# One decoder step on one core: the S5 direct term moved into the Toeplitz matrix, and an S5 plan with other prices

## The chip, the cores and the metric

The kernel runs as one launch on one core of a Trainium2 chip. The metric is device time in microseconds (us), the median of several executions. TensorE (PE, with its weight loads as PEld), VectorE (DVE), ScalarE (ACT), GpSimd (POOL) and SyncE (SP) each work through a queue of their own, in order. All DMAs of this kernel are issued from SP's queue.

## What is computed

One layer of a hybrid decoder, for 512 prompt tokens and 8 sample tokens, which the kernel holds side by side as 520 columns. The input projection feeds two branches: an S5 state space model (64 groups of 16 channels with 64 complex states) and a Mamba-2 SSD. The change touches the S5 branch alone:

```python
h_re, h_im = associative_scan(...)                  # h_t = abar h_(t-1) + bbar u_t
y = einsum("ghn,blgn->blgh", c_re, h_re) - einsum("ghn,blgn->blgh", c_im, h_im)
y = y + d_skip * u32                                # the direct term
ya = gelu(y)
out = ya * sigmoid(ya @ w_glu + b_glu)
```

Behind it come the SSD branch, gates on both, an output projection, and a SwiGLU feed-forward part.

## The kernel before, in words

**Big products.** Every projection is cut into tiles of 128 output channels by 520 columns. A weight tile of 128x1024 is loaded, split by ACT into a rounded high part (`whi`, line 755 `acp`) and by DVE into the rest (`wlo`, line 699 `vtt`), and PE multiplies it with the high and low parts of the activations (`hi`, `lo`): six matmuls of 260 columns for each of 8 slices of the contraction, 48 for a tile, all recorded at line 782 (`mm`). The results go to one of two PSUM tiles, `pm`, and are read out by ACT or DVE. These products run in a fixed list of tiles: 8 tiles `u` (the S5 input), a small `dt` tile, then sixteen gate tiles and four SSD groups of ten tiles (`B`, `C`, four `xs`, four `z`). `CUT` (line 513) says how many gate tiles stand ahead of the first group and behind each group: with `[12, 14, 16, 16, 16]` it is 12 ahead, 2 behind the first group and 2 behind the second. Then come `glu`, `bs5`, `bssd`, `wo`, the feed-forward tiles `fg`/`fu` and `fo`. What a tile costs besides its products depends on its kind. A gate is copied out by ACT and stored by a DMA. A `B`, `C` or `xs` tile is copied out twice by ACT and gets a convolution from three DVE instructions of line 710 (`stt`), 509 to 511 columns each. A `z` tile goes through SiLU on ACT.

**S5.** The prompt is split into 64 blocks of 8 steps, and channels are handled in 8 units `q` of 8 groups. `s5_prep` builds a unit's matrices; among them a Toeplitz matrix T that maps the 8x16 inputs of a block to its outputs. It arises from `KP`, whose part `[:, :, 112:]` is copied from PSUM by ACT, written to DRAM and read back eight times in shifted form (`kd`). `s5_load` reorders the unit's input (an ACT copy with a strided side, `acp` of `uv`) and sends it through DRAM (`ud`). `s5_body` runs the state scan on DVE (`scan`, line 722), then two matmuls per group, T on the input and C on the entering state (73 columns each, into a `bank` of PSUM). The result goes through DRAM (`yd`) to come back in the layout of `u`, and two DVE instructions (`stt`, line 710) add `D u` in place: one for 512 prompt columns, read with a stride, and one for 8 sample columns. `s5_tabs` builds tables of powers for two units at a time; ACT fills them with 64x8 copies, and three DMAs per unit spread them out. When all 8 units are done, `gelu` runs over the S5 output in two ACT instructions of 2080 columns.

**SSD.** A group's first matmuls are transposes of its `B`, C and `xs` tiles (`tp`, line 794), which need their SiLU from ACT. Sixteen `ssd_unit`s accumulate with DVE instructions of 64 columns (line 710). `ygsplit` splits the 16 result tiles for `bssd`.

**The order.** The program is recorded once with estimated durations. `Plan.order` then gives each operation a priority, lays them out engine by engine (`play`), rates the layout with late DMAs (`rehearse`) and keeps the best of 61 perturbed tries. So a changed cost in a helper, or a changed list of operations, gives every engine another order from the start. The estimates of the operations that the change touches are, in microseconds: `scan` .068 + columns/960; `stt` .068 + columns/960 (+ .061); `acp` .052 + columns/1200 (+ .042).

In the profile, `s`, `arena`, `hi`, `lo`, `whi`, `wlo` are SBUF, `pm` and `bank` PSUM, and one line stands for all uses of a helper: 699 `vtt`, 710 `stt`, 716 `vcp` (a copy that the planner gives to DVE or ACT), 722 `scan`, 750 `act`, 755 `acp`, 771 `dma`, 782 `mm`, 794 `tp`.

Of the kernel before, what the change touches and what calls it, by code (L numbers as in the profile page):

```python
# [14 lines left out]
MULT, ADD, SUB, MIN, MAX = ALU.mult, ALU.add, ALU.subtract, ALU.min, ALU.max  # L15

NP, NS = 512, 8
# [7 lines left out]
C2 = TWO_PI - C1  # L25
MAGIC = 12582912.0

V_NPM, V_NPO, V_NPF, V_NPOF, V_BADA, V_S5D, V_BGLU, V_CONVB, V_MNORM, V_MD, V_CONVW, V_N = (
    0, 8, 16, 24, 32, 80, 88, 96, 120, 136, 152, 248)
K_ID, K_MASK, K_ONE, K_SGN, K_NSGN, K_N = 0, 128, 256, 384, 385, 386  # L30


# [477 lines left out]
NHALF = 4  # L510
NLAST = 2
THIRD = ("fg", 4)
CUT = [12, 14, 16, 16, 16]


class Arena:
# [143 lines left out]
class Builder:  # L660
# [58 lines left out]
        self.op("V", .068 + self.fs(o) / 160, lambda: self.nc.vector.reciprocal(out=real(o), in_=real(a)), [o], [a])  # L719

    def scan(self, o, a, b):
        self.op("V", .068 + self.fs(o) / 960, lambda: self.nc.vector.tensor_tensor_scan(
            out=real(o), data0=real(a), data1=real(b), initial=0.0, op0=MULT, op1=ADD), [o], [a, b])

    def vred(self, o, a):
# [24 lines left out]
        self.op("A", c, lambda: self.nc.scalar.activation(real(o), real(a), f, bias=real(bias), scale=real(scale)),  # L750
                [o], [a, scale, bias], None if free else f)

    def acp(self, o, a):
        c = self.act_cost(o, a)
        self.op("A", c, lambda: self.nc.scalar.copy(real(o), real(a)), [o], [a])  # L755

    def dma(self, o, a, boost=0.0):
# [1242 lines left out]
    def s5_prep(self, q, un, KP, BB32):  # L2000
        I = self.I
        t = self.s5t
        gs = slice(8 * q, 8 * q + 8)
        pm, sw, bb = yield from self.ring("tmp", q, 1, [512, 128, 1024])
        un["Cs"], bst = yield from self.ring("set", q, NSET, [1152, 2048])
        un["Bst"], un["T"] = bst.ap[:, :1024], bst.ap[:, 1024:]
        pv = pm.v(4, 8, 16)
        td = self.dma(pm.v(512), I["s5m"][q])
        wv = un["Bst"][:, :512].rearrange("p (a b c) -> p a b c", a=4, b=8)
        Bsw = sw.v(8, 16)  # L2010
        V = self.vtt
        BX, BY, CX, CY = [pv[:, i] for i in range(4)]
        sgn = self.cst[:, K_SGN:K_SGN + 1]
        yield td

        Bb = BB32[:, :, :16]
        f2 = lambda i: bc(t["F"][:, i:i + 2, gs], 3, 16)
        V(wv[:, 0:2], pv[:, 0:2], f2(0), MULT)
        V(wv[:, 2:4], pv[:, 0:2], f2(2), MULT)
        cs, bbv = un["Cs"].v(8, 9, 16), bb.v(8, 8, 16)  # L2020
        V(Bb, wv[:, 0], wv[:, 1], ADD)
        self.acp(bbv[:, :, 7], Bb)
        V(Bsw, wv[:, 3], wv[:, 2], SUB)
        self.act(CY, CY, AF.Copy, scale=-1.0)
        self.act(CX, CX, AF.Copy, scale=self.cst[:, K_NSGN:K_NSGN + 1])
        self.acp(cs[:, :, 0], CX)
        yield "c"
        b7, c8 = bbv[:, :, :7], cs[:, :, 1:]
        t3, t4 = un["Bst"].rearrange("p (a b c) -> p a b c", a=8, b=8), un["T"][:, :896].rearrange("p (a b c) -> p a b c", a=8, b=7)
        pj = lambda a: bc(a[:, :, gs].rearrange("p j g -> p g j"), 3, 16)  # L2030
        V(t3, pj(t["PIM"][:, 1:]), bc(CY, 2, 8), MULT)
        V(c8, pj(t["PRE"][:, 1:]), bc(CX, 2, 8), MULT)
        yield "c"
        V(c8, c8, t3, ADD)
        yield 0
        V(t4, pj(t["DIM"]), bc(Bsw, 2, 7), MULT)
        V(b7, pj(t["DRE"]), bc(Bb, 2, 7), MULT)
        yield "c"
        V(b7, b7, t4, ADD)
        yield 0  # L2040
        for h in range(2):
            p = yield from self.pget()
            with self.bunch():
                for i in range(4):
                    self.tp(p[:, i * 128:(i + 1) * 128], bb.v(8, 128)[:, 4 * h + i], 128)
            yield 0
            self.acp(un["Bst"][:, 512 * h:512 * h + 512], p)
# [12 lines left out]
        yield 0  # L2060
        td = self.dma(kd.rearrange("(r j) h w -> (j h) r w", r=2), KP)
        self.done.add(("s5v", q))
        yield td
        Tt = un["T"].rearrange("p (a b) -> p a b", a=8)
        for j in range(8):
            td = self.dma(Tt[16 * j:16 * j + 16], kd.rearrange("g h w -> h g w")[:16, :, 112 - 16 * j:240 - 16 * j])
        yield td
        self.done.add(("s5p", q))

    def s5_load(self, q, un, U, Hm):  # L2070
# [5 lines left out]
        I = self.I  # L2076
        u = self.ub.v(KD, T)[:, q]
        uv = up.v(T)
        self.acp(uv[:, :NP].rearrange("p (s c) -> p s c", s=8), u[:, :NP].rearrange("p (c s) -> p s c", s=8))
        self.acp(uv[:, NP:], u[:, NP:])  # L2080
        ud = self.udd[q % 2]
        self.dma(Hm[:, :, 65:73], I["s5hx"][:, gs])
# [5 lines left out]
        td = self.dma(ud[0][:, 73:81], uv[:, NP:])  # L2088
# [12 lines left out]
    def s5_body(self, q, un, U, Hm):  # L2101
        nc, I, O = self.nc, self.I, self.O
        t = self.s5t
        u = self.ub.v(KD, T)[:, q]
        gs = slice(8 * q, 8 * q + 8)
        hs, d0, yb = un["ld"]
        a, b = yield from self.ring("ab", q, 1, [512, 512])
        bst = un["Bst"].rearrange("p (a b) -> p a b", a=8)
        vps = []
        for h in range(2):  # L2110
            p = yield from self.pget()
# [8 lines left out]
        for h in range(2):  # L2120
            s4 = slice(4 * h, 4 * h + 4)
            vp, p = vps[h]
# [18 lines left out]
        for h in range(2):  # L2141
            p = yield from self.pget()
# [14 lines left out]
        td = self.dma(yd, yb.v(584))  # L2157
        yv = yb.ap[:, :T]
        yield td
        yt = yd.rearrange("(t h) (g c) -> (h g) t c", t=8, g=8)  # L2160
        self.dma(yv[:, :NP].rearrange("p (t c) -> p t c", t=8), yt[:, :, :64])
        yield self.dma(yv[:, NP:], yt[:, 0, 65:])
        d = self.vec[:, V_S5D + q:V_S5D + q + 1]
        un_ = u[:, :NP].rearrange("p (c s) -> p c s", s=8)
        self.stt(un_, un_, d, yv[:, :NP].rearrange("p (s c) -> p c s", s=8), MULT, ADD)
        self.stt(u[:, NP:], u[:, NP:], d, yv[:, NP:], MULT, ADD)
        self.rfree("ld", q, 2)
        self.done.add(("s5", q))

# [307 lines left out]
def layout(inputs):  # L2477
    import numpy as np
    a = {k: np.asarray(v) for k, v in inputs.items()}
    f = np.ascontiguousarray  # L2480

    def fm(v):
        return f(v.reshape(-1, 128).T)

    def wt(w):
# [3 lines left out]
    d = {}  # L2489
    x = np.concatenate([a["x_prompt"][0], a["x_sample"][:, 0]], 0)  # L2490
    d["xT"] = f(x.T.reshape(8, 128, T).transpose(1, 0, 2))
    c = np.zeros((32, 1024), np.float32)
# [13 lines left out]
    cw = np.concatenate([fm(a["m_conv_w"][0][k]) for k in range(4)], 1)  # L2506
    d["vec"] = f(np.concatenate([
        fm(a["norm_pre_mix"][0]), fm(a["norm_post_mix"][0]), fm(a["norm_pre_ffn"][0]), fm(a["norm_post_ffn"][0]),
        fm(a["b_ada"][0]), fm(a["s5_d"][0][per]), fm(a["s5_b_glu"][0][per]), fm(a["m_conv_b"][0]), fm(a["m_norm"][0]),
        fm(np.repeat(a["m_d"][0], 64)), cw], 1))  # L2510
    lr, li, ld = a["s5_lam_re"][0], a["s5_lam_im"][0], a["s5_log_dt"][0]
    ldr = np.broadcast_to(ld[:, None], (64, 64))
# [1 line left out]
    br, bi = a["s5_b_re"][0].transpose(1, 0, 2), a["s5_b_im"][0].transpose(1, 0, 2)  # L2514
    cr, ci = a["s5_c_re"][0].transpose(2, 0, 1), a["s5_c_im"][0].transpose(2, 0, 1)
    m4 = np.stack([np.concatenate(v, 0) for v in ((br, bi), (bi, br), (cr, ci), (ci, cr))], 1)
    d["s5m"] = f(m4.reshape(128, 4, 8, 8, 16).transpose(2, 0, 1, 3, 4).reshape(8, 128, 512))
    sr, si = a["state_s5_re"][0].transpose(2, 1, 0), a["state_s5_im"][0].transpose(2, 1, 0)
    d["s5hx"] = f(np.concatenate([sr, si], 0))
    d["s5hy"] = f(np.concatenate([si, sr], 0))  # L2520
# [8 lines left out]
    for g in range(4):  # L2529
        o = 3072  # L2530
# [48 lines left out]
```

## Time and profile before

| what | value |
|---|---|
| time, median of 3 runs | 1185.79 us (1185.43 to 1188.05) |
| the profiled execution, its own time | 1188.7 us |
| its span, first to last instruction | 1186.6 us |
| PE busy | 1163.7 us, 98% |
| DVE busy | 811.7 us, 68% |
| ACT busy | 569.1 us, 48% |
| mean granted TensorE clock | 0.997 |

The profile gives busy times per engine, a table by stretches of time, the waits of each engine with what ended them, a chain of work that ended last, groups of equal instructions, and a timeline. A busy PE is not one at its peak, since its matmuls overlap: in a steady stretch a matmul of 260 columns is recorded with some 280 ns but a new one starts every 0.12 us.

### The profile page before, as it was taken

The numbers are of one execution on the slowest core, as the hardware profiler recorded it, in microseconds if no ns is written. First come the engines' busy times: TensorE is split into PE (matmuls) and PEld (weight loads), VectorE is DVE, ScalarE is ACT, GpSimd is POOL, SyncE is SP. The second block draws the span as 40 slices with busy tenths as digits, with TensorE's granted clock in tenths as the row PEclk, the third lists the DMA queues.
The fourth block names the chain that finished last, engine by engine and source line by source line (L and its number), as shares of the span: only waits on it lengthen the run. The fifth ranks groups of instructions, "written<-read, shape, count | busy, mean of one in ns | idle before, by whom it ended". The sixth has DMA issues, their size and how long they took to land.

```text
span 1186.6 us, 24809 instructions
## 1 busy us (share of the span) xinstructions
PE 1163.7 (98%) x10182; PEld 1125.9 (95%) x10182; DVE 811.7 (68%) x1629; ACT 569.1 (48%) x996; POOL 4.8 (0%) x32
## 2 busy tenths in 40 slices
PE   8999999899999999999999999999999999999997
PEld 6899999898999999999998989999999999999997
DVE  6798699998975976879974334399676773322236
ACT  5766335447685574768862223466222223222233
POOL 0000000000000000000000000000000000000000
PEclk9999999999999999999999999999999999999999
DMA  9858579676443533446465665434566663222344
GB/s 293 280 145 202 166 193 181 147 208 185 133 132 114 177 112 117 143 147 200 139 209 187 238 218 196 174 92 150 180 198 214 188 225 107 85 85 81 98 118 133
DMA packets 118065, 195.48 MB, mean 165 GB/s; under 512 B 45856, under 2 KB 68800, under 8 KB 115648
## 3 DMA queue, kind: packets, MB, share of 16 engines
q1 hardware_dynamic: 117952, 193.90, 54.0%
q8 instruction: 80, 1.31, 0.5%
q14 instruction: 33, 0.27, 0.1%
HBM read 165.81 MB, written 23.86 MB: 160 GB/s over the span
## 4 chain that ended last, share of the span: by engine, by line
PE 72%; DVE 3%; ACT 1%; issue 1%; DMA 0%; DVEq 0%; SPq 0%
PE pm L782 60%; PE bank L782 11%; DVE s L699 1%; PE bank L794 1%; DVE arena L699 1%; DMA arena<-in_w_fi 0%; ACT s L750 0%; ACT L750 0%; DVE arena L710 0%; DVE lo L710 0%; ACT arena L750 0%; DVE arena L719 0%; ACT whi L755 0%; ACT s L755 0%; DVE s L710 0%
## 5 line engine op out<-in xcount | busy, mean ns | idle before, releaser
L782 PE MATMUL pm<-hi,whi 128*128 128x260 f32 (+1 forms) x1856 | 496.6, 289 | 4.3 <-ACT s L750 3.8
L782 PE MATMUL pm<-lo,whi 128*128 128x260 f32 (+1 forms) x1856 | 484.4, 283 | 0.6 <-DVE lo L710 0.6
L782 PE MATMUL pm<-hi,wlo 128*128 128x260 f32 x1840 | 371.0, 283 | 0.7 <-DVE wlo L699 0.7
L782 PEld LDWEIGHTS pm<-hi,whi 128*128 128x128 f32 (+1 forms) x1856 | 350.0, 189 | 13.9 <-issue 8.6
L782 PEld LDWEIGHTS pm<-lo,whi 128*128 128x128 f32 (+1 forms) x1856 | 349.7, 188 | 1.1 <-DVE lo L710 1.0
L699 DVE TENSOR_TENSOR wlo<-arena,whi 128x1024 fp32r<-128x1024 f32 (+1 forms) x157 | 188.8, 1204 | 157.0 <-ACT whi L755 154.6
L782 PEld LDWEIGHTS pm<-hi,wlo 128*128 128x128 f32 x1840 | 283.7, 189 | 0.9 <-DVE wlo L699 0.9
L755 ACT CAST whi<-arena 128x1024 fp32r<-128x1024 f32 (+1 forms) x158 | 162.6, 1029 | 223.3 <-PE pm L782 212.0
L782 PE MATMUL pm<-s,whi 128*128 128x260 f32 (+2 forms) x1128 | 184.3, 284 | 0.0
L699 DVE TENSOR_TENSOR arena<-arena 128x512 f32<-128x512 f32 (+11 forms) x298 | 138.7, 491 | 37.6 <-DMA arena<-in_ssm 18.9
L782 PEld LDWEIGHTS pm<-s,whi 128*128 128x128 f32 x1128 | 156.1, 188 | 6.0 <-issue 5.9
L782 PE MATMUL pm<-s,wlo 128*128 128x260 f32 (+2 forms) x564 | 117.1, 282 | 0.0
L782 PEld LDWEIGHTS pm<-s,wlo 128*128 128x128 f32 x564 | 88.1, 188 | 0.0
L750 ACT ACTIVATE s<-s 128x520 f32<-128x520 f32 (+11 forms) x102 | 60.5, 599 | 43.8 <-DVE s L699 28.7
L782 PE MATMUL bank<-s,s 128*64 128x128 f32 (+5 forms) x696 | 78.8, 281 | 1.5 <-ACT s L755 1.1
L699 DVE TENSOR_TENSOR s<-s,s 128x512 f32<-128x512 f32 (+9 forms) x120 | 76.7, 654 | 3.7 <-ACT s L750 2.9
L750 ACT ACT_TABLE_LOAD x56 | 71.8, 1283 | 10.0 <-DMA s<-acd 7.9
L782 PEld LDWEIGHTS bank<-s,s 128*128 128x128 f32 (+2 forms) x696 | 65.2, 166 | 5.2 <-ACT s L755 1.4
L750 ACT ACTIVATE arena<-pm 128x260 f32<-128x260 f32 (+3 forms) x43 | 20.6, 485 | 92.3 <-PE pm L782 86.7
L699 DVE TENSOR_TENSOR s<-arena,s 128x520 fp32r<-128x520 f32 (+5 forms) x60 | 56.7, 947 | 7.5 <-ACT s L755 5.4
L699 DVE TENSOR_TENSOR arena<-arena,pm 128x520 f32<-128x520 f32 x26 | 18.1, 696 | 54.3 <-PE pm L782 54.2
L782 PE MATMUL bank<-hi,s 128*128 128x260 f32 x256 | 54.4, 285 | 0.6 <-ACT s L755 0.6
(122 smaller groups left out, 1259.0 us busy)
## 6 DMA issues: line engine op xcount, KB each, us to landing
arena<-in_w_in SPq DMA_DIRECT2D x59, 512.0 KB, 4.2
arena<-in_w_fi SPq DMA_DIRECT2D x44, 512.0 KB, 3.5
arena<-in_w_ada SPq DMA_DIRECT2D x12, 1024.0 KB, 6.3
arena<-in_w_fo SPq DMA_DIRECT2D x20, 512.0 KB, 3.5
s<-acd SPq DMA_DIRECT2D x16, 512.0 KB, 4.0
arena<-in_ssmT SPq DMA_DIRECT2D x16, 512.0 KB, 4.5
arena<-in_w_bssd SPq DMA_DIRECT2D x16, 512.0 KB, 4.4
arena<-in_ssm SPq DMA_DIRECT2D x32, 256.0 KB, 3.8
```

Of the source, the lines that this page charges most:

```text
L699: self.op("V", .068 + self.fs(o) / 960, lambda: self.nc.vector.tensor_tensor(out=real(o), in0=real(a), in1=real(b), op=op), [o], [a, b, *a ...
L750: self.op("A", c, lambda: self.nc.scalar.activation(real(o), real(a), f, bias=real(bias), scale=real(scale)), [o], [a, scale, bias], None ...
L755: self.op("A", c, lambda: self.nc.scalar.copy(real(o), real(a)), [o], [a])
L782: self.pe(c, lambda: self.nc.tensor.matmul(real(o), lhsT=real(l), rhs=real(r), start=start, stop=stop), [o], [l, r], 128 if m > 64 or l.dt ...
L794: self.pe(.112, lambda: self.nc.tensor.transpose(real(o), real(a), real(d)), [o], [a, d])
```

## The change

Three things. The D of each channel is added on the diagonal of `KP`'s first block, before that goes to DRAM: the Toeplitz matmul then yields `D u` with the rest. D arrives as 32 more columns of the DMA `s5m`. The two DVE instructions at the end of `s5_body` go; in their place ACT copies the 512 prompt columns from `yd`'s return into `u`, and the DMA of the 8 sample columns writes into `u` itself. The planner's costs of `scan` and of the strided ACT copies are raised. `CUT` becomes `[16, 16, 16, 16, 16]`: all gate tiles stand ahead of the first SSD group.

```diff
-V_NPM, V_NPO, V_NPF, V_NPOF, V_BADA, V_S5D, V_BGLU, V_CONVB, V_MNORM, V_MD, V_CONVW, V_N = (
-    0, 8, 16, 24, 32, 80, 88, 96, 120, 136, 152, 248)
+V_NPM, V_NPO, V_NPF, V_NPOF, V_BADA, V_BGLU, V_CONVB, V_MNORM, V_MD, V_CONVW, V_N = (
+    0, 8, 16, 24, 32, 80, 88, 112, 128, 144, 240)
...
-CUT = [12, 14, 16, 16, 16]
+CUT = [16, 16, 16, 16, 16]
...
     def scan(self, o, a, b):
-        self.op("V", .068 + self.fs(o) / 960, lambda: self.nc.vector.tensor_tensor_scan(
+        self.op("V", .068 + self.fs(o) / 480, lambda: self.nc.vector.tensor_tensor_scan(
...
-    def acp(self, o, a):
-        c = self.act_cost(o, a)
+    def acp(self, o, a, more=0.0):
+        c = self.act_cost(o, a) + more
...
# s5_prep
-        pm, sw, bb = yield from self.ring("tmp", q, 1, [512, 128, 1024])
+        pm, sw, bb = yield from self.ring("tmp", q, 1, [544, 128, 1024])
...
-        td = self.dma(pm.v(512), I["s5m"][q])
+        td = self.dma(pm.ap[:, :544], I["s5m"][q])
...
         self.acp(KP[:, :, 112:], p[:, :256].rearrange("p (a b) -> p a b", a=2))
         self.pfree(p)
+
+        self.vtt(KP[:, :, 112:128], KP[:, :, 112:128], dk, ADD)
...
# s5_load
-        self.acp(uv[:, :NP].rearrange("p (s c) -> p s c", s=8), u[:, :NP].rearrange("p (c s) -> p s c", s=8))
+        self.acp(uv[:, :NP].rearrange("p (s c) -> p s c", s=8), u[:, :NP].rearrange("p (c s) -> p s c", s=8), .62)
...
# s5_body
-        yield self.dma(yv[:, NP:], yt[:, 0, 65:])
-        d = self.vec[:, V_S5D + q:V_S5D + q + 1]
-        un_ = u[:, :NP].rearrange("p (c s) -> p c s", s=8)
-        self.stt(un_, un_, d, yv[:, :NP].rearrange("p (s c) -> p c s", s=8), MULT, ADD)
-        self.stt(u[:, NP:], u[:, NP:], d, yv[:, NP:], MULT, ADD)
+        yield self.dma(u[:, NP:], yt[:, 0, 65:])
+        self.acp(u[:, :NP].rearrange("p (c s) -> p c s", s=8), yv[:, :NP].rearrange("p (s c) -> p c s", s=8), .62)
```

Two places in the order. On PE, around the first matmuls of the first SSD group: the row with `8x128` and the rows `bank<-arena,s_... 128x128 x4` are its transposes, rows with `whi` and `wlo` are big products. Before, within a `pm_70` tile:

```order
L794 MATMUL bank_67<-arena 128x128 x4
L782 MATMUL pm_70<-hi,whi_72 128x260
L782 MATMUL pm_70<-lo,whi_72 128x260
L782 MATMUL pm_70<-hi,whi_72 128x260
L782 MATMUL pm_70<-lo,whi_72 128x260
L782 MATMUL pm_70<-hi,wlo_75 128x260 x2
L794 MATMUL bank_68<-arena,s_23_829 128x128 x4
L782 MATMUL bank_66<-s_22_2322,s_13_594 128x128 x4
L782 MATMUL bank_65<-s_16_875,arena 32x128 x8
```

Now:

```order
L794 MATMUL bank_66<-arena,s_32_2541 8x128
L782 MATMUL pm_70<-hi,whi_72 128x260
L782 MATMUL pm_70<-lo,whi_72 128x260
L782 MATMUL pm_70<-hi,whi_72 128x260
L782 MATMUL pm_70<-lo,whi_72 128x260
L782 MATMUL pm_70<-hi,wlo_75 128x260 x2
L782 MATMUL pm_69<-hi,whi_71 128x260
L782 MATMUL pm_69<-lo,whi_71 128x260
L782 MATMUL pm_69<-hi,whi_71 128x260
L782 MATMUL pm_69<-lo,whi_71 128x260
L782 MATMUL pm_69<-hi,wlo_74 128x260 x2
L794 MATMUL bank_65<-arena,s_32_2541 128x128 x4
```

The first of these transposes stood behind 1614 big matmuls of 260 columns and stands behind 1866 now; S5's last Toeplitz matmul went from behind 1848 to behind 2016, the last SSD matmul from behind 3480 to behind 3570.

On ACT, around the first half of the GELU (the row with `128x2080`), with SiLUs of SSD tiles (`s_23`, `s_33`), reads of `pm`, and casts to `whi`. Before:

```order
L716 COPY arena<-s_23_829 128x8
L750 ACT_TABLE_LOAD
L750 ACTIVATE arena<-arena 128x2080
L755 COPY s_14_692<-bank_68 128x292
L750 ACT_TABLE_LOAD
L750 ACTIVATE s_23_829<-s_23_829 128x520
L755 COPY s_14_692<-bank_66 128x292
L750 ACTIVATE s_14_692<-pm_69,arena 128x520
L755 COPY s_13_594<-pm_69 128x520
L755 CAST whi_71<-arena 128x1024
```

Now:

```order
L755 COPY arena<-s_18_1182 128x512
L755 COPY arena<-arena 128x8x63
L755 COPY arena<-bank_68 128x2x128
L750 ACT_TABLE_LOAD
L750 ACTIVATE arena<-arena 128x2080
L755 CAST whi_71<-arena 128x1024
L750 ACTIVATE s_33_835<-pm_70,arena 128x520
L755 COPY s_32_2541<-pm_70 128x520
```

The half stood between two SiLUs of the first SSD group; it stands now behind one of the new copies into `u` (`arena<-s_18_1182 128x512`), ahead of a cast and the reads of `pm_70`, and no SiLU follows it in these rows. Over the whole program ACT has 64 table loads where it had 56, and DVE 1647 instructions where it had 1631.

## Rows read from the trace of the kernel before

**Rows 1.** The page, busy time of each engine, share of the span, instructions
```profile
PE 1163.7 (98%) x10182; PEld 1125.9 (95%) x10182; DVE 811.7 (68%) x1629; ACT 569.1 (48%) x996; POOL 4.8 (0%) x32
```

**Rows 2.** Table by stretches: length, busy PE, PEld, DVE, ACT, POOL; clock, DMA
```profile
60.00:150.00 90.00, 88.19 (x783) 85.47 (x782) 74.15 (x202) 47.88 (x115) 1.33 (x7) 1.00 0.67 173
150.00:215.00 65.00, 63.38 (x565) 61.75 (x564) 62.94 (x111) 30.74 (x71) 0.60 (x6) 1.00 0.82 174
215.00:280.00 65.00, 61.25 (x531) 60.37 (x530) 64.25 (x121) 27.12 (x63) 0.56 (x5) 0.97 0.75 197
280.00:310.00 30.00, 27.64 (x245) 26.46 (x243) 24.66 (x57) 26.13 (x41) 0.00 (x0) 0.94 0.56 151
310.00:600.00 290.00, 290.00 (x2807) 283.01 (x2806) 231.88 (x525) 199.43 (x298) 0.32 (x1) 1.00 0.45 142
```

**Rows 3.** Waits of PE over the whole span: total, times, longest
```profile
PE pm L782 <- ACT s L750: 3.8, 1, 3.8
...
PE bank L794 <- ACT s L716: 2.4, 1, 2.4
```

**Rows 4.** Timeline of PE behind its first long wait: start, length, instruction
```profile
225.24 0.39 PE L782 MATMUL pm<-hi,whi 128*128 128x260 f32 x1 [3.75 <-ACT s L750]
...
227.09 0.42 PE L782 MATMUL pm<-hi,whi 128*128 128x260 f32 x1
...
228.38 0.42 PE L782 MATMUL pm<-hi,whi 128*128 128x260 f32 x1
...
230.47 0.28 PE L782 MATMUL pm<-hi,whi 128*128 128x260 f32 x1
...
231.19 0.28 PE L782 MATMUL pm<-hi,whi 128*128 128x260 f32 x1
```

**Rows 5.** Timeline of ACT in the same place
```profile
223.56 0.20 ACT L755 COPY s<-arena 64x8 f32<-64x8 f32 x1 [4.79 <-DMA s<-s]
223.78 0.59 ACT L755 COPY s<-pm 128x520 f32<-128x520 f32 x1
224.40 0.79 ACT L750 ACTIVATE s<-pm,arena 128x520 f32<-128x520 f32 x1
```

**Rows 6.** The chain that ended last, 276 to 291 us: start, length, what
```profile
276.24 1.19 DVE arena L710 x2
277.43 1.22 DVE s L699 x2
...
280.62 1.28 ACT L750
...
284.16 1.28 ACT L750
...
290.05 0.12 ACT s L716
290.17 0.04 issue
290.21 0.66 PE bank L794 x4
```

**Rows 7.** Groups of DVE up to 470 us, by shape: busy, mean ns, idle before
```profile
L699 DVE TENSOR_TENSOR wlo<-arena,whi 128x1024 fp32r<-128x1024 f32 x55 | 67.0, 1218 | 14.8 <-ACT whi L755 14.5
...
L710 DVE SCALAR_TENSOR_TENSOR s<-s,arena,s 128x511 f32<-128x511 f32 x15 | 11.2, 747 | 2.8 <-ACT s L750 1.8 <-ACT s L755 0.9
...
L710 DVE SCALAR_TENSOR_TENSOR arena<-arena,s 128x512 f32<-128x512 f32 x8 | 9.1, 1136 | 0.1
...
L722 DVE TENSOR_TENSOR_SCAN s<-arena,s 128x512 f32<-128x512 f32 x4 | 4.9, 1219 | 0.0
...
L699 DVE TENSOR_TENSOR s<-s,bank 128x32 f32<-128x32 f32 x16 | 2.7, 181 | 0.2
...
L710 DVE SCALAR_TENSOR_TENSOR arena<-arena,s 128x8 f32<-128x8 f32 x8 | 1.7, 218 | 0.0
```

**Rows 8.** Groups of ACT up to 470 us, by shape
```profile
L755 ACT COPY s<-bank 128x512 f32<-128x512 f32 x21 | 12.1, 583 | 3.6 <-DVE s L699 2.3 <-PE bank L794 1.2 <-PE bank L782 0.2
...
L755 ACT COPY s<-arena 128x512 f32<-128x512 f32 x8 | 9.7, 1215 | 1.8 <-DVE arena L705 1.2 <-DMA ud<-s 0.6
```

**Rows 9.** DMA issues by line: count, KB each, median us to landing
```profile
s<-in_s5m SPq DMA_DIRECT2D x8, 256.0 KB, 3.5
...
s<-yd SPq DMA_DIRECT2D x8, 256.0 KB, 4.9
```

**Rows 10.** Timeline: DVE's last SSD accumulations
```profile
594.68 0.46 DVE L710 SCALAR_TENSOR_TENSOR arena<-arena,s,bank 128x64 f32<-128x64 f32 x2
```

**Rows 11.** Timeline: PE's first product of `bssd`
```profile
631.70 0.52 PE L782 MATMUL pm<-s,whi 128*128 128x260 f32 x3
```

More of the change, by code (lines that the diff above doesn't have):

```diff
@@ L2003, in s5_prep @@
         gs = slice(8 * q, 8 * q + 8)
-        pm, sw, bb = yield from self.ring("tmp", q, 1, [512, 128, 1024])
+        pm, sw, bb = yield from self.ring("tmp", q, 1, [544, 128, 1024])
         un["Cs"], bst = yield from self.ring("set", q, NSET, [1152, 2048])
         un["Bst"], un["T"] = bst.ap[:, :1024], bst.ap[:, 1024:]
-        pv = pm.v(4, 8, 16)
-        td = self.dma(pm.v(512), I["s5m"][q])
+        pv, dk = pm.ap[:, :512].rearrange("p (a b c) -> p a b c", a=4, b=8), pm.ap[:, 512:544].rearrange("p (a b) -> p a b", a=2)
+        td = self.dma(pm.ap[:, :544], I["s5m"][q])
         wv = un["Bst"][:, :512].rearrange("p (a b c) -> p a b c", a=4, b=8)
@@ L2508, in layout @@
         fm(a["norm_pre_mix"][0]), fm(a["norm_post_mix"][0]), fm(a["norm_pre_ffn"][0]), fm(a["norm_post_ffn"][0]),
-        fm(a["b_ada"][0]), fm(a["s5_d"][0][per]), fm(a["s5_b_glu"][0][per]), fm(a["m_conv_b"][0]), fm(a["m_norm"][0]),
+        fm(a["b_ada"][0]), fm(a["s5_b_glu"][0][per]), fm(a["m_conv_b"][0]), fm(a["m_norm"][0]),
         fm(np.repeat(a["m_d"][0], 64)), cw], 1))
@@ L2516, in layout @@
     m4 = np.stack([np.concatenate(v, 0) for v in ((br, bi), (bi, br), (cr, ci), (ci, cr))], 1)
-    d["s5m"] = f(m4.reshape(128, 4, 8, 8, 16).transpose(2, 0, 1, 3, 4).reshape(8, 128, 512))
+    m4 = m4.reshape(128, 4, 8, 8, 16).transpose(2, 0, 1, 3, 4).reshape(8, 128, 512)
+    dk = np.zeros((8, 4, 32, 2, 16), np.float32)
+    h = np.arange(16)
+    dk[:, :, h, :, h] = a["s5_d"][0].reshape(8, 2, 4, 16).transpose(3, 0, 2, 1)
+    d["s5m"] = f(np.concatenate([m4, dk.reshape(8, 128, 32)], 2))
     sr, si = a["state_s5_re"][0].transpose(2, 1, 0), a["state_s5_im"][0].transpose(2, 1, 0)
```

## The prediction, made before the changed kernel was run

> **What bounds the kernel now.** I read the page's busy times first: PE is busy in 98% of the span, DVE in 68%, ACT in 48% [rows 1]. As matmuls overlap, that says that PE hardly ever stands still, not that it is at its peak. The matmuls of the big products are as many after the change as before, so the time can fall only where PE idles or where its clock is low, and can rise wherever a new wait reaches PE. So the table by stretches came next, read for the difference between length and busy PE [rows 2]. From 310 to 600 us it is nothing. From 60 to 310 us it is 1.8, 1.6, 3.8 and 2.4 us, 9.5 in all; between 150 and 280 us DVE is busy 62.9 and 64.3 of 65 us, so there DVE, with S5's work upon it, comes near to setting the pace. In the last two stretches the granted clock falls to 0.97 and 0.94.
>
> The waits name two events [rows 3]: 3.8 us on a `pm` and 2.4 us on a `bank` of the transposes. The timelines show how the first arises [rows 4, 5]: ACT stood 4.79 us before a 64x8 table copy, which waited for a DMA, and the two reads of `pm`, queued behind it and long due, came late. No DVE work stands in that wait. The second is followed back in the chain of waits [rows 6]: DVE ends the two additions of `D u` (276.24, 1.19 us) and its work behind them, ACT then loads a table, runs the GELU half, loads a table again at 284.16, and gets to the small copy at 290.05 that the first SSD transposes need.
>
> Each event costs more than its wait. Behind the first, six matmuls took 228.38 - 227.09 = 1.29 us, and a little later 231.19 - 230.47 = 0.72 us [rows 4]: the lower of the clock's two levels, 1.2 GHz, and then the upper, 2.4. PE had just stood still for 3.75 us. The stretch means give 2 x 0.03 x 65 = 3.9 and 2 x 0.06 x 30 = 3.6 us at the low level [rows 2], both from rounded means; I take 3.4. The loss is 3.4 x (1 - 0.72/1.29) = 1.5 us each. (The Trainium skill, "TensorE: Matmul & The Clock Gate", section "HAM oscillation — how this bites in real kernels", counts the loss as throttled time times 1 - 1.2/2.4, half and not 44%; by that it would be 1.7 us each, 0.4 us more in the sum; the row, taken over whole matmuls with their issue, decides.)
>
> **The change, part by part.** *DVE, removed and added.* Eight additions over 512 columns at 1136 ns and eight over 8 at 218 go: 9.1 + 1.7 = 10.8 us. Eight additions into `KP` of 2x16 = 32 columns come; the nearest row is 128x32 with one operand in PSUM, 181 ns [rows 7]: 8 x 0.18 = 1.5 us. An unshown strided form might cost as little as 0.1 or as much as the 218 ns row: 0.8 to 1.7. Net -9.3 us, all between some 60 and 300 us. None of it is PE time; it is worth something only where PE waits for DVE.
>
> *ACT, added.* Eight copies of 512 columns with a strided side. `s5_load` makes the same reordering in the other direction, at 1215 ns; a plain 512 column copy from PSUM takes 583 [rows 8]. I take the first, as it also has the stride: 9.7 us, bounds 4.7 and 9.7. ACT is busy 30.7 and 27.1 of 65 us in the S5 stretches [rows 2], so the time is covered. Its order is not: a copy waits for the DMA that returns `yd`, median 4.9 us [rows 9], and behind it in ACT's queue stand reads of `pm` and the casts to `whi`, for which PE waits. Before, that wait was DVE's. ACT also gets eight more table loads at 1.28 us [rows 6], 10.3 us, likewise covered by its idle half, if none stands ahead of a needed read.
>
> *DMA.* `s5m` grows from 256 to 272 KB, at 3.5 us a piece [rows 9] that is 0.2 us, eight times, fetched long ahead: nothing. The return of the 8 sample columns stays one DMA on SP; it writes into `u` in place of `yv`, with no new wait. But the `gelu` and the last reader of old `u` now order that DMA; nothing is queued for it alone.
>
> *CUT.* Four gate tiles come ahead of the first group. A tile is 48 matmuls at 0.12 us [rows 4], 5.8 us of PE; four are 23 us. A gate owes DVE one split of 1.22 us; a `B`, `C` or `xs` tile owes that and three convolution steps of 0.75 [rows 7]. So over the stretch in which S5 must be finished, four tiles with 2.24 us of DVE more are exchanged for four without: about 9 us less. Together with the 9.3 that is some 18 us of DVE relief in a stretch of 130 us where it was 98% busy, hence down to about 85%; at 80% (231.9 of 290 us) PE lost nothing [rows 2]. It is not lost, since the convolutions come after 310 us, where 58 us of DVE are idle. The order agrees: the first transposes come 252 matmuls, about 30 us, later, S5's last Toeplitz matmul 168, about 20 us.
>
> *The plan's prices.* A scan was planned at 0.60 us and takes 1.22; a `D u` addition at 0.66 and takes 1.14 [rows 7]; the strided copy at 0.52, 1.22 in the trace [rows 8]. The old plan ran some 1.7 us short in every unit, 14 us over eight, so that the order was made for a DVE that was not there. The new one errs less. This carries no term of its own; it is why I trust that the waits named above go and few come.
>
> *The two waits.* The first hung on ACT's queue order around one DMA. In the new order every S5 step stands elsewhere, so that meeting does not recur as it was: 3.75 + 1.5 = 5.25 us. The second hung on the GELU standing between SiLUs of the first group. In the new order the transposes stand behind 30 us more of PE work, while S5 ends 20 us later in matmuls; so 10 us of slack and more, against a wait of 2.4: 2.4 + 1.5 = 3.9 us. What is late next: waits of the small kind. Between 60 and 215 us they are 1.8 + 1.6 = 3.4 us in 155 us; S5 now lasts through the 90 us or so that were the two events' stretch, and 3.4/155 x 90 = 2.0 us come back.
>
> Sum: -5.25 - 3.9 + 2.0 = -7.1 us. The profiled execution took 1188.7 us, 1186.6 of span and 2.1 around it; so 1181.6. The median of the runs is 2.9 below the profiled one: 1185.8 - 7.1 = **1178.7**.
>
> **The rivals.** *No change* (1185.8). PE is at 98%, and all that the change cuts is DVE's; the stalls were accidents of an in-order queue, and a whole new order brings as many accidents elsewhere: -9.1 + 9.1. For it: the first wait was not DVE's at all [rows 5]. Against: DVE's 98% stretch is eased, and where it was at 80%, no accident reached PE in 290 us [rows 2]. (The Trainium skill, "Perfetto Trace Analysis", section "Identifying the Most-Contended Engine", says to work on the engine with the highest occupancy first; by it this change treats the wrong engine and gives nothing. The stretches disagree: 9.5 us of PE idle lie where DVE is at its limit.)
>
> *The SSD comes too late for `bssd`.* DVE's last accumulation started at 594.68 and `bssd` at 631.70 [rows 10, 11]: some 37 us between, part of which the `ygsplit`s need. The last SSD matmul moves by 90 matmuls, 11 us; were the whole 30 us of the start carried through, 7 would be left. A wait there decides only beyond 37; were it 44, 7 us would be lost and the time about 1185.8 again. Against: gates that went ahead leave the end of the list no longer.
>
> *Slower: ACT takes DVE's place.* Eight copies wait on `yd` in ACT's queue, which the reads of `pm` share. One that comes too early does what the table copy did: 3.75 us and a low clock, 5.25 us [rows 4, 5]. It needs more than 7.1/5.25, so two such meetings for no gain, and (7.1 + 2.4)/5.25 = 1.8 to be slower than the measurement can hide: with two, 1178.7 + 10.5 = 1189.2. For it: it happened once before at a queue with fewer such waits, and the added table loads lengthen them. Against: ACT is half idle, and the DMA's 4.9 us is known to be there when the order is made.
>
> **How the numbers follow.** Differences within 0.2%, 2.4 us, are about what a measurement of this kernel can tell from none. Forecast 0.62, no change 0.15, late `bssd` 0.05, slower 0.18. Below lies at most the case in which every idle microsecond from 60 to 310 us goes: 9.5 + 3.0 = 12.5, 1173.3. Above, the range takes in the two meetings, 1189.2; left out are three and more of them (about 0.1) and a gain over 12.5 us (0.05).
>
> **What would show it.** Right: no PE wait above 1.5 us between 60 and 330 us, granted clock 1.00 in these stretches, DVE clearly below 95% between 150 and 280 us, the group of DVE additions with 512 columns gone and eight ACT copies near 1.2 us in its place, no wait of `bssd`. Wrong: a PE wait on `pm` or `whi` that ACT released after waiting for `s<-yd` (the third rival); PE idle on `bank` of the SSD or of `bssd` (the second); the same 9 us in several waits of 0.5 to 2 us (the first).

## The result, and the profile of the changed kernel

| | median | lowest to highest | ratio to before, 95% interval |
|---|---|---|---|
| before | 1186.92 us (4 runs) | 1185.43 to 1188.11 | |
| changed | 1179.42 us (4 runs) | 1177.74 to 1181.29 | 0.9939 [0.9925, 0.9953] |

The gain is 0.61%, 7.2 us of the 1186.9, between 5.6 and 8.9. The forecast had been 7.1. The profiled execution of the changed kernel took 1177.86 us, with a span of 1175.8, so 10.8 us less than that of before; the median moved less, since two of the four runs lie near 1181.1, at a mean granted clock of 0.995 to 0.996, and two near 1177.8, at 0.998 to 0.999.

The page's busy times of the changed kernel, to be read against [rows 1]:

```profile
PE 1162.2 (99%) x10182; PEld 1123.6 (96%) x10182; DVE 806.7 (69%) x1645; ACT 583.5 (50%) x988; POOL 4.8 (0%) x32
```

PE has the same 10182 matmuls and is busy 1.5 us less; what changed is the time between them. The table by stretches, as [rows 2] (the granted clock is the third number from the end):

```profile
60.00:150.00 90.00, 90.00 (x803) 87.88 (x802) 74.49 (x203) 47.50 (x111) 1.69 (x9) 1.00 0.64 166
150.00:215.00 65.00, 63.80 (x572) 62.54 (x571) 61.95 (x120) 31.53 (x69) 0.67 (x6) 1.00 0.84 205
215.00:280.00 65.00, 64.60 (x569) 63.69 (x568) 61.41 (x117) 40.20 (x85) 0.56 (x5) 1.00 0.70 182
280.00:310.00 30.00, 30.00 (x267) 29.64 (x266) 23.82 (x50) 24.00 (x37) 0.00 (x0) 1.00 0.64 177
310.00:600.00 290.00, 290.00 (x2824) 282.72 (x2823) 238.97 (x556) 208.35 (x289) 0.32 (x1) 1.00 0.45 145
```

PE idles 0 + 1.2 + 0.4 + 0 = 1.6 us between 60 and 310 us where it idled 9.5, and the granted clock is 1.00 throughout where two stretches had 0.97 and 0.94. From 310 on it is fed without a gap, as before. But the DVE column hardly moved: 62.0 and 61.4 of 65 us, against 62.9 and 64.3. The waits of PE between 60 and 310 us (total, times, longest) are all there is left of [rows 3]:

```profile
PE bank L782 <- DVE s L699: 1.2, 1, 1.2
PE bank L794 <- DVE s L699: 0.4, 1, 0.4
```

The groups of DVE and ACT show the exchange that the change makes, at the durations of [rows 7, 8]: the additions into `KP`, and ACT's copies into `u` below those of `s5_load`:

```profile
L699 DVE TENSOR_TENSOR arena<-arena,s 128x32 f32<-128x32 f32 x8 | 1.5, 184 | 0.0
```

```profile
L755 ACT COPY s<-arena 128x512 f32<-128x512 f32 x8 | 9.5, 1193 | 5.1 <-DMA ud<-s 4.3 <-DVE arena L705 0.8
L755 ACT COPY arena<-s 128x512 f32<-128x512 f32 x8 | 9.1, 1135 | 4.5 <-DMA s<-yd 4.5
```

ACT did wait 4.5 us in all for the return of `yd`, but no wait of PE follows from it. DVE's last SSD accumulation (against 594.68 in [rows 10]) and PE's first product of `bssd` (against 631.70 in [rows 11]) stand at:

```profile
583.91 0.46 DVE L710 SCALAR_TENSOR_TENSOR s<-s,s,bank 128x64 f32<-128x64 f32 x2
```

```profile
618.25 0.64 PE L782 MATMUL pm<-s,whi 128*128 128x260 f32 x4
```

So 34 us lie between, where 37 did.

### The profile page after: what moved, and what is told of

Same layout as the page of the kernel before. It is cut to its first block, busy times and chain, and to the rows that moved or that the text cites. A ratio compares the mean times of both kernels' runs of the same rounds, so it can differ in the third digit from the quotient of the medians.

```text
span 1175.8 us, 24819 instructions
## 1 busy us (share of the span) xinstructions
PE 1162.2 (99%) x10182; PEld 1123.6 (96%) x10182; DVE 806.7 (69%) x1645; ACT 583.5 (50%) x988; POOL 4.8 (0%) x32
## 4 chain that ended last, share of the span: by engine, by line
PE 84%; DVE 7%; DMA 4%; issue 1%; SPq 1%; ACT 1%; DVEq 0%; ACTq 0%
PE pm L782 70%; PE bank L782 13%; DVE s L699 3%; PE bank L794 2%; DMA s<-in_w_as 1%; DVE arena L699 1%; SPq L771 1%; DMA s<-kd 1%; DMA s<-in_w_in 1%; DMA arena<-in_w_in 1%; DVE wlo L699 1%; DVE arena L719 0%; DVE s L710 0%; DMA ud<-s 0%; DVE lo L710 0%
## 5 line engine op out<-in xcount | busy, mean ns | idle before, releaser
L782 PE MATMUL pm<-hi,whi 128*128 128x260 f32 x1856 | 495.5, 288 | 0.2 <-ACT arena L755 0.2
L782 PE MATMUL pm<-lo,whi 128*128 128x260 f32 x1856 | 483.4, 282 | 0.2 <-DVE lo L710 0.2
L782 PEld LDWEIGHTS pm<-hi,whi 128*128 128x128 f32 x1856 | 349.1, 188 | 9.1 <-issue 8.0
L782 PEld LDWEIGHTS pm<-lo,whi 128*128 128x128 f32 x1856 | 348.7, 188 | 0.6 <-DVE lo L710 0.4
L699 DVE TENSOR_TENSOR arena<-arena 128x512 f32<-128x512 f32 (+12 forms) x302 | 141.7, 497 | 26.7 <-ACT arena L750 12.2
L699 DVE TENSOR_TENSOR s<-s,s 128x512 f32<-128x512 f32 (+10 forms) x118 | 65.1, 559 | 8.7 <-ACT s L750 7.2
L750 ACT ACTIVATE s<-s 128x520 f32<-128x520 f32 (+9 forms) x91 | 47.2, 524 | 38.2 <-DVE s L699 20.8
L699 DVE TENSOR_TENSOR s<-arena,s 128x520 fp32r<-128x520 f32 (+5 forms) x60 | 56.4, 948 | 11.5 <-ACT s L755 10.7
L782 PE MATMUL bank<-s,s 128*32 128x128 f32 (+4 forms) x664 | 59.1, 279 | 1.2 <-DVE s L699 1.2
L782 PEld LDWEIGHTS bank<-s,s 128*128 128x128 f32 (+1 forms) x664 | 52.2, 154 | 3.4 <-DVE s L699 1.3
L782 PE MATMUL pm<-hi,s 128*128 128x260 f32 x256 | 54.8, 285 | 0.3 <-ACT arena L750 0.3
```

The costliest lines, as they stand in the source:

```text
L782: self.pe(c, lambda: self.nc.tensor.matmul(real(o), lhsT=real(l), rhs=real(r), start=start, stop=stop), [o], [l, r], 128 if m > 64 or l.dt ...
```

## The experiments

Each kernel stands beside runs of the kernel before on the same chip. "PE idle" is the length less busy PE from 60 to 310 us, "DVE" its busy time there, both of the profiled execution.

| kernel | median us | ratio, 95% interval | PE idle | DVE |
|---|---|---|---|---|
| before | 1186.9 | | 9.5 | 226.0 |
| changed | 1179.4 | 0.9939 [0.9925, 0.9953] | 1.6 | 221.7 |
| h1: lighter additions, old order | 1182.3 | 0.9963 [0.9952, 0.9975] | 6.5 | 224.5 |
| h2: table copy freed, old order | 1186.8 | 0.9996 [0.9987, 1.0004] | 9.1 | 226.4 |
| h12: both, old order | 1181.6 | 0.9953 [0.9941, 0.9966] | 5.6 | 225.5 |
| h3: DVE work put back, new order | 1188.6 | 1.0010 [0.9995, 1.0024] | 5.6 | 225.5 |
| D u alone | 1185.5 | 0.9988 [0.9980, 0.9997] | 7.9 | 223.4 |
| CUT alone | 1187.1 | 0.9999 [0.9990, 1.0008] | 7.9 | 221.3 |
| prices alone | 1182.0 | 0.9958 [0.9945, 0.9971] | 2.3 | 233.5 |
| D u and CUT | 1183.4 | 0.9983 [0.9963, 1.0003] | 4.9 | 215.9 |
| D u and prices | 1181.1 | 0.9955 [0.9941, 0.9970] | 5.4 | 222.7 |
| before, other seed | 1187.7 | 1.0008 [0.9997, 1.0020] | 6.3 | 229.2 |
| prices alone, other seed | 1183.7 | 0.9970 [0.9958, 0.9982] | 4.1 | 233.2 |
| changed, other seed | 1179.9 | 0.9941 [0.9928, 0.9953] | 3.0 | 218.9 |

### With the order held

In the first four kernels plan and order are those of before or of after; only what an operation carries out is another. h1 leaves out `D u` on most columns of the S5 output, h2 one column of the tables of six units, h12 both.

**h1.** Before, with the additions on 8 columns instead of 512:

```diff
-        self.stt(un_, un_, d, yv[:, :NP].rearrange("p (s c) -> p c s", s=8), MULT, ADD)
+        yn_ = yv[:, :NP].rearrange("p (s c) -> p c s", s=8)
+        self.op("V", .068 + self.fs(un_) / 960 + .061, lambda: self.nc.vector.scalar_tensor_tensor(
+            out=real(un_[:, :1]), in0=real(un_[:, :1]), scalar=real(d), in1=real(yn_[:, :1]), op0=MULT, op1=ADD),
+            [un_], [un_, d, yn_])
```

> The kernel before, with its plan and order untouched; the eight additions of D u over 512 columns are carried out on 8 columns only (the rest of the S5 output lacks D u), so DVE is relieved of about 8 x 0.92 = 7.4 us at the old places. Theory (PE waits where DVE is at its limit, and the second wait of PE hangs on the last of these additions): the wait of 2.4 us on the bank of the first SSD transposes and its low clock go, the wait of 3.8 us on pm stays; -3.9 us, about 1183. Rival (only the new order matters, DVE's relief is nothing): within 1 us of the kernel before, and the 2.4 us wait is still there.

It took 0.9963 of before, 4.4 us less, close to the 3.9 expected. The wait at the SSD transposes is gone (no PE idle from 280 to 310 us, clock 1.00), and the other one stays. The table by stretches:

```profile
215.00:280.00 65.00, 61.38 (x533) 60.51 (x532) 61.65 (x126) 31.70 (x68) 0.56 (x5) 0.97 0.75 200
280.00:310.00 30.00, 30.00 (x276) 29.20 (x276) 25.82 (x62) 24.86 (x40) 0.00 (x0) 1.00 0.56 158
```

The first row of its waits of PE over the whole span:

```profile
PE pm L782 <- ACT s L750: 3.6, 1, 3.6
```

So the second term of the sum stood on the right chain: the additions of `D u` did delay the first transposes.

**h2.** Before, with the 64x8 copies of three of the four pairs of units writing where no DMA reads:

```diff
-                self.acp(pln[h, 1, :, 1], t["c8"][h, gs])
-                self.acp(pln[h, 2, :, 1], t["s8"][h, gs])
+                for j, k in ((1, "c8"), (2, "s8")):
+                    o, x = pln[h, j, :, 1], t[k][h, gs]
+                    self.op("A", self.act_cost(o, x), lambda o=o, x=x, q=q: self.nc.scalar.copy(
+                        real(x if q else o), real(x)), [o], [x])
```

> The kernel before, with its plan and order untouched; the 64x8 table copies of the second, third and fourth pair of units no longer write into the table that a DMA still reads (they copy their input onto itself, so the tables of these units are wrong in one column). Theory (the wait of 3.8 us on pm is ACT standing before that copy, and costs 3.75 and 1.5 for the clock): -5.25 us, about 1181, the 2.4 us wait stays. Rival (accidents: what is not late here is late a little further on): less than 2.5 us gained, with a new wait of PE over 1 us within the next 30 us.

Nothing was gained that shows: 0.9996, with an interval from a loss of 0.5 us to a gain of 1.5. ACT's timeline shows that the edit did what it should: the copy runs without a wait, and the reads of `pm` start at 217.85, where they stood at 223.78 in [rows 5]:

```profile
217.63 0.20 ACT L1974 COPY arena<-arena 64x8 f32<-64x8 f32 x1
217.85 0.59 ACT L755 COPY s<-pm 128x520 f32<-128x520 f32 x1
218.47 0.78 ACT L750 ACTIVATE s<-pm,arena 128x520 f32<-128x520 f32 x1
```

PE's wait of 3.75 us is gone, and others have come, on DVE and on an ACT copy of S5, with a clock of 0.83 between 230 and 240 us:

```profile
233.18 1.08 PE L794 MATMUL bank<-arena 128*128 128x128 f32 x4 [1.58 <-DVE arena L699]
...
257.08 1.11 PE L782 MATMUL bank<-s,s 128*128 128x72 f32 x8 [1.48 <-ACT s L755]
```

```profile
230.00:240.00 10.00, 8.42 (x72) 7.96 (x71) 10.00 (x22) 6.02 (x15) 0.00 (x0) 0.83 0.44 129
```

The last row is of the table by stretches; DVE is busy all of these 10 us. From 215 to 280 us PE now idles 3.3 us where it idled 3.75 [rows 2]: what the table copy no longer holds up stands behind DVE and ACT a little later. The rival was right here, and the forecast's term of 5.25 us for this wait was wrong.

**h12.** Both edits.

> Both edits at once, still in the order of before. Theory: the two waits are separate, their prices add: -9.1 us, about 1177, which is as fast as the changed kernel or faster, without its new order. Rival: the gains do not add, and 1180 or more is left.

0.9953, so 5.6 us gained [4.0 to 7.0] where 9.1 were expected: the rival's side, though not for its reason. The gains measured singly, 4.4 and 0.5, do add up to about this; what is wrong is the size of the first, 5.25. Against h1 alone (0.9963) the intervals overlap: with the additions light, the table copy is worth some 1.2 us, by a difference that could as well be nothing.

**h3.** The changed kernel, with two more DVE instructions in the operation that adds into `KP`:

```diff
-        self.vtt(KP[:, :, 112:128], KP[:, :, 112:128], dk, ADD)
+        o, x = KP[:, :, 112:128], dk
+
+        def add(o=o, x=x):
+            self.nc.vector.tensor_tensor(out=real(o), in0=real(o), in1=real(x), op=ADD)
+            for _ in range(2):
+                self.nc.vector.scalar_tensor_tensor(out=real(KP), in0=real(KP), scalar=1.0, in1=real(KP), op0=MULT, op1=MAX)
+        self.op("V", .068 + self.fs(o) / 960, add, [o], [o, x])
```

> The changed kernel, with its plan and order untouched; behind each addition into KP stand two more DVE instructions over 480 columns (KP = max(KP, KP)), some 1.45 us a unit, 11.6 us in all: DVE has as much to do as before, a little more. Theory (the relief of DVE is what keeps PE supplied): waits of PE come back between 100 and 300 us, and 3 to 9 us are lost. Rival (the gain comes from the order, the relief adds nothing): within 1.5 us of the changed kernel.

1188.6 us: 9.2 more than the changed kernel, so the whole gain is lost, for 817.4 - 806.7 = 10.7 us of DVE work; the twelve runs spread from 1183.3 to 1191.4. One wait of 3.05 us on S5 came back, and behind it a low clock (0.66 over 10 us); from 140 to 160 us two waits of 0.55 and 1.01 came with 0.91. PE's timeline, and two rows of the table by stretches:

```profile
147.59 0.44 PE L794 MATMUL bank<-arena,s 128*128 128x128 f32 x2 [0.55 <-DVE s L722]
149.04 0.33 PE L794 MATMUL bank<-arena,s 128*128 128x128 f32 x1 [1.01 <-DVE s L699]
...
250.43 0.44 PE L782 MATMUL bank<-s,arena 128*128 128x73 f32 x2 [3.05 <-DVE s L699]
```

```profile
140.00:160.00 20.00, 18.44 (x154) 17.72 (x153) 17.78 (x36) 9.41 (x24) 0.11 (x1) 0.91 0.63 168
250.00:260.00 10.00, 9.57 (x55) 9.57 (x56) 9.84 (x16) 3.25 (x11) 0.11 (x1) 0.66 0.81 196
```

The DVE instruction that ended the wait of 3.05 us stood right behind the two added ones in DVE's queue:

```profile
248.43 1.35 DVE L2064 SCALAR_TENSOR_TENSOR arena<-arena 128x480 f32<-128x480 f32 x2
249.69 0.69 DVE L699 TENSOR_TENSOR s<-s 128x512 f32<-128x512 f32 x1
```

Taken alone this says that the relief of DVE is the gain. The next kernels, which plan anew, say that it isn't so simple.

### The parts, each planned anew

**D u alone**: the diff without the line of `CUT`, without the new cost of `scan`, and with no `.62` on the two strided copies.

> The kernel before with D u through the Toeplitz matmuls alone (KP's diagonal, eight copies on ACT in place of the sixteen DVE additions); CUT and the plan's prices as before, planned anew. Theory after the runs with the order held (DVE's load in the S5 stretch decides, and 7.4 us less of it were worth 4.6 us): 4 to 6 us gained, about 1182. Rival 1 (the prices make the plan, and without them the new copies are planned too short and meet reads of pm): no gain or a loss, with a PE wait that ACT released behind s<-yd. Rival 2 (CUT does it): less than 2 us gained.

1.4 us gained [0.4 to 2.4], at most a third of what was expected. The number is on the side of rival 2, whose reason, `CUT`, the next kernel refutes; the sign of rival 1 did not come, as ACT waits for `yd` 0.2 us in all. PE still idles 7.9 us from 60 to 310 us, in eight waits of at most 1.8, though the two big waits are gone (waits of PE in that stretch, the four costliest):

```profile
PE bank L782 <- ACT s L755: 2.5, 3, 1.3
PE bank L782 <- DVE s L699: 2.0, 2, 1.8
PE bank L782 <- ACT arena L755: 1.5, 1, 1.5
PE bank L794 <- DVE s L722: 1.4, 1, 1.4
```

**CUT alone**:

```diff
-CUT = [12, 14, 16, 16, 16]
+CUT = [16, 16, 16, 16, 16]
```

> The kernel before with CUT = [16, 16, 16, 16, 16] alone, planned anew. Theory: it puts off about 9 us of DVE's convolution work until S5 is done, worth as much as the same relief elsewhere where it falls behind the place of the first wait: 2 to 4 us gained, about 1184, with the wait at the first SSD transposes gone and waits near 220 us left. Rival (it is the whole gain): 7 us. Rival (nothing, as the convolutions fill the gaps that S5 leaves): within 1.5 us of before.

Nothing: 0.9999, as the last rival has it. DVE has 4.7 us less to do from 60 to 310 us than before, and PE idles 7.9 us.

**Prices alone**:

```diff
     def scan(self, o, a, b):
-        self.op("V", .068 + self.fs(o) / 960, lambda: self.nc.vector.tensor_tensor_scan(
+        self.op("V", .068 + self.fs(o) / 480, lambda: self.nc.vector.tensor_tensor_scan(
...
-        self.acp(uv[:, :NP].rearrange("p (s c) -> p s c", s=8), u[:, :NP].rearrange("p (c s) -> p s c", s=8))
+        self.acp(uv[:, :NP].rearrange("p (s c) -> p s c", s=8), u[:, :NP].rearrange("p (c s) -> p s c", s=8), .62)
```

> The kernel before with the plan's new prices alone (the scan, and the strided copy of s5_load, at their traced durations), planned anew. Theory: no work is taken off DVE, so 0 to 2 us gained, about 1186. Rival (the old order failed because it was made for a DVE that was not there): 4 us or more gained, fewer waits of PE between 100 and 300 us.

The rival was right: 5.0 us gained [3.4 to 6.5], though not one instruction was taken off DVE. The table by stretches of this kernel:

```profile
60.00:150.00 90.00, 90.00 (x818) 88.05 (x817) 85.45 (x222) 52.32 (x126) 1.54 (x9) 1.00 0.79 192
150.00:215.00 65.00, 65.00 (x576) 64.39 (x575) 64.32 (x114) 32.78 (x75) 0.83 (x8) 1.00 0.81 194
215.00:280.00 65.00, 62.71 (x534) 61.02 (x533) 56.57 (x114) 29.98 (x66) 0.11 (x1) 0.95 0.73 186
```

From 60 to 215 us DVE is busy 149.8 of 155 us, more than before (137.1), and PE does not wait once. A DVE at its limit is thus not enough to make PE wait. What moves is seen at the scans. Of the eight over 512 columns, the first and the fourth, in the kernel before:

```profile
136.81 1.22 DVE L722 TENSOR_TENSOR_SCAN s<-arena,s 128x512 f32<-128x512 f32 x1
...
206.70 1.22 DVE L722 TENSOR_TENSOR_SCAN s<-s,s 128x512 f32<-128x512 f32 x1
```

and with the prices alone:

```profile
121.68 1.22 DVE L722 TENSOR_TENSOR_SCAN s<-arena,s 128x512 f32<-128x512 f32 x1
...
186.99 1.22 DVE L722 TENSOR_TENSOR_SCAN s<-s,s 128x512 f32<-128x512 f32 x1
```

The first four scans run 15 to 20 us earlier, in the time in which DVE of the old order had been idle: 15.9 us of 90 from 60 to 150 us [rows 2], now 4.6. But an early S5 is not the gain. `D u` alone, at the old prices, has the same two scans as early:

```profile
121.83 1.22 DVE L722 TENSOR_TENSOR_SCAN s<-arena,s 128x512 f32<-128x512 f32 x1
...
190.06 1.22 DVE L722 TENSOR_TENSOR_SCAN s<-s,s 128x512 f32<-128x512 f32 x1
```

It gained 1.4 us. The changed kernel has them at 139.20 and 193.55, with DVE idle for 15.5 us from 60 to 150 us, nearly as long as before, and gained 7.2. What the changed kernel shares with the prices alone is few waits of PE.

By the Trainium skill, "DVE: opcode table, instruction layouts, handler registers and perf-mode slots", section "6. Datapath and trigger behaviour", the built-in scan runs at half throughput. The trace agrees, column for column: a scan of 128 columns takes 0.42 us and one of 512 takes 1.22, so 2.1 ns for each column more, where the products and sums of line 699 take 0.68 us for 512 columns and 1.22 for 1024, so some 1.05 ns.

**D u and CUT, without the prices.**

> The changed kernel without the new prices (scan and strided copies as before), planned anew. Theory: as fast as the changed kernel within 2 us, about 1180. Rival (prices): 1183 or more.

1183.4 us, the rival's side of its bound, but twelve runs spread from 1180.6 to 1192.7 and the interval reaches 1.0003. Its median is 4 us above the changed kernel's, and the two intervals do not overlap, so the prices do a good part here too.

**D u and prices, without CUT.**

> The changed kernel with CUT as before (D u through the Toeplitz matmuls, and the new prices), planned anew. Theory after the runs of the single parts (the prices order the queues so that PE is fed, -5; D u takes 9 us off DVE and adds the rest, CUT nothing): as fast as the changed kernel within 2 us, about 1180, with at most 2.5 us of PE idle between 60 and 310 us. Rival (CUT is needed once D u is off DVE): 1183 or more.

0.9955, the same as the prices alone (0.9958). So on top of the prices `D u` adds nothing that shows without `CUT`, and `CUT` adds some 1.9 us to the two, with intervals that overlap. At most 2.5 us of PE idle were expected; the profile has 5.4, and it is that of the longest of its six runs, 1184.7.

### Other draws of the plan

A changed cost gives another order, and one order may simply be luckier. The seed of the perturbed tries was changed from 149 to 150 in three kernels.

> The kernel before, planned from another random seed: the same work and prices, other perturbed tries. Theory (the old prices make orders that starve PE, whichever try wins): within 2 us of before, 1185 to 1189, with 6 us or more of PE idle between 60 and 310 us. Rival (the order of before was one unlucky draw): 1183 or less.

> The kernel before with the new prices alone, planned from another random seed. Theory (right prices, not a lucky draw): 1180.5 to 1184, with 3 us of PE idle or less between 60 and 310 us. Rival (lucky draw): 1185 or more.

> The changed kernel, planned from another random seed. Theory: 1178 to 1182. Rival (the order of the changed kernel is a lucky draw): 1184 or more.

All three came out on the theory's side: 1.0008, 0.9970 and 0.9941, where the first seed had 1, 0.9958 and 0.9939. In these three a draw moved the time by 0.2 to 1.4 us; the three kinds of kernel keep their distance. Only the idle time of the middle one, 4.1 us, was larger than expected.

**What follows.** Four pairs of kernels differ by the prices alone, and in each the two intervals lie apart: the prices gain 5.0 us on the kernel before, 4.5 on it with the other seed (1.0008 to 0.9970), 3.9 with `D u` (0.9988 to 0.9955) and 5.2 with `D u` and `CUT` (0.9983 to 0.9939). `D u` and `CUT` together add 2.3 us on the first seed (0.9958 to 0.9939, intervals overlapping) and 3.4 on the second (0.9970 to 0.9941, intervals apart). Neither of the two shows more than 1.4 us by itself. So most of the gain comes from costs in the planner, and not from the work that was taken off DVE. Prices with `CUT` but without `D u` were not run, nor the price of `scan` apart from that of the copy, so which of each pair carries the effect stays open.

One reading joins these runs with h1, h12 and h3: what costs is time that the plan does not know of, on DVE and ACT together. As an estimate from planned costs and traced durations, the kernel before is planned some 14 us short over its eight units (on DVE 0.62 a scan and 0.48 an addition, on ACT 0.70 a strided copy). `D u` alone and `D u` with `CUT` are some 16 short, as a second strided copy on ACT comes in, and h3 is some 12.5 short. These, with h2, `CUT` alone and the other seed of before, gain 2.0 us at most or lose. h1 and h12 are some 7 short, the prices alone 5, the changed kernel with or without `CUT` 2; they gain 3.6 to 7.2. DVE's part alone does not sort them: it is 5.6 us for `D u` alone and 4.5 for the prices alone, which gained 1.4 and 5.0. Nor does the load: the kernel with the prices alone has 814.7 us of DVE work, the changed one 806.7, and they are 2.3 us apart. Within either group the gain does not follow the size. That the surprise is the cause is therefore argued and not shown; no run varied the error of the plan alone in steps.

## Why the prediction was right, and where not

The time (1178.7 forecast, 1179.4 measured), the sign and the range held. The steps behind it held only in part, and that the sum came out so close is luck: a term that was too large stood in for one that was left out.

- *What bounds the kernel.* Right: nothing could be won but PE's idle time from 60 to 310 us and the low clock there. Between the two profiled executions, 10.8 us apart, 7.9 us are idle time in that stretch, and two spells of low clock, at the forecast's 1.5 us each, make 3.0 more; the rest of the span nets almost nothing.
- *What comes back.* Too much was put back: of the 9.5 us of idle time 5.4 were to stay or return, and in the profiled execution it is 1.6. The median agrees all the same, because it stands 1.6 us above that execution. One loss was not foreseen: in that execution the clock falls at the end, and from the last group of six matmuls on it needs 11.7 us where that of before needed 10.7. The last stretches of the changed kernel, and a group of four matmuls there on the timeline:

```profile
1160.00:1170.00 10.00, 8.35 (x52) 7.24 (x52) 6.54 (x22) 2.21 (x8) 0.00 (x0) 0.86 0.33 111
1170.00:1175.80 5.80, 1.80 (x6) 0.90 (x4) 0.98 (x3) 1.32 (x4) 0.00 (x0) 0.79 0.53 181
```

```profile
1168.73 1.91 PE L782 MATMUL pm<-arena 128*128 128x256 f32 x4
```

Before, four such matmuls took some 1.0 us:

```profile
1180.04 0.59 PE L782 MATMUL bank<-arena 128*128 128x256 f32 x2
1180.47 0.59 PE L782 MATMUL pm<-arena 128*128 128x256 f32 x2
```

- *The term of the second wait*, 3.9 us: right in mechanism and size (h1: 4.4).
- *The term of the first wait*, 5.25 us: the wait went, but its price was wrong. h2 took it away alone and gained 0.5 us, by an interval that takes in nothing; DVE and ACT were late for PE right behind it. What ended a wait is not yet what set it.
- *"This carries no term of its own"*, said of the plan's prices: the step that failed most. They are the largest part, 3.9 to 5.2 us in four pairs of kernels. The numbers were there: 0.62, 0.48 and 0.70 us are 1.8 us short in every unit (the prediction has 1.7), 1.1 of it DVE's and 0.7 ACT's. The new prices take back 0.53 of a scan and 0.62 of each strided copy.
- *D u and CUT* were to relieve DVE from 98 to about 85% of the S5 stretches and so to free PE. DVE stayed at 95% (62.0 and 61.4 of 65), so the sign "clearly below 95%" did not come: the new order fills the place with other work. Part of that work is new on DVE. The planner gives it 76 of the small copies of line 716 where it had 51, 13.4 us where it had 8.9, and so DVE's total fell by 5.0 us and not by 9.3. Alone `D u` and `CUT` gave 1.4 and 0.1 us, which with 5.0 for the prices makes 6.5 of the 7.2 measured. The total of the forecast agreed because the first wait, taken for 5.25 us and worth 0.5, stood in for the prices, taken for nothing.
- *ACT's side and the DMAs* were right: 1.14 us a copy (1.2 taken), 184 ns an addition (180 taken), no wait of PE from `yd`, no wait at `bssd`.
- *The rivals.* "No change" was refuted as an outcome, but its mechanism, one stall in the place of another, is what h2 and the kernel with `D u` alone show: the waits that were to go went, and others came. The late `bssd` and the meetings on ACT did not occur.
- By the Trainium skill, "Perfetto Trace Analysis", section "Identifying the Most-Contended Engine", the engine with the highest occupancy is to be optimized first. The prediction read this as speaking against the change, and that reading was wrong. The engine is PE, at 98%, and it is PE's own idle time that the change took away, 7.9 us of it from 60 to 310 us, by way of the order of DVE's and ACT's work.

## What to carry to other kernels

Where an order is planned ahead, compare each planned cost with the traced duration first: here two corrected prices alone, with no work taken away, gave most of the gain. A wait removed by itself is worth its length only if nothing else is late just behind it; try it with the order held before the length goes into a sum. And when the change plans anew, run its parts and a second seed before crediting any one of them.

## What the runs showed of the chip

The low clock does not go by the length of one wait. In h3 waits of 0.55 and 1.01 us within 2 us were followed by 0.91 over 20 us. The changed kernel had a wait of 1.20 us at 169 us, and that with `D u` alone eight waits of up to 1.8 us from 60 to 310 us; both kept 1.00 there. Nor does it go by the place. At the first SSD transposes PE waited 2.4 us before and 2.5 us in h2; before, the clock was 0.94 from 280 to 310 us [rows 2], in h2 it was 1.00:

```profile
289.10 0.66 PE L794 MATMUL bank<-arena,s 128*128 128x128 f32 x4 [2.49 <-ACT s L716]
```

```profile
280.00:310.00 30.00, 27.51 (x253) 26.45 (x253) 24.88 (x61) 26.23 (x39) 0.00 (x0) 1.00 0.63 171
```

At the very end the kernel before and the changed one have the same two waits, 1.10 and 0.51 us. Behind the second, two matmuls took 0.70 us before and 1.22 in the changed kernel, at granted clocks of 1.00 and 0.66 over 5 us:

```profile
1179.51 0.70 PE L782 MATMUL pm<-arena 128*128 128x256 f32 x2 [0.51 <-DVE arena L699]
```

```profile
1167.71 1.22 PE L782 MATMUL bank<-arena 128*128 128x256 f32 x2 [0.51 <-DVE arena L699]
```

By the Trainium skill, "TensorE: Matmul & The Clock Gate", section "HAM oscillation — how this bites in real kernels", waits between groups of matmuls bring the clock down and cost half of the throttled time. That the clock falls behind waits these traces show, but not behind every wait of a length. Of the time at the low level 44% was lost here, and not half: six matmuls took 1.29 us at that level and 0.72 at the upper one [rows 4]. The mean granted clock of one and the same program, the changed kernel, lay between 0.995 and 0.999 in its four executions.
